# Eight matmuls on a tile of zeros ahead of all others on TensorE, in a transformer block on one core

## The chip, the cores and the metric

One Trainium2 chip, one of its cores. The metric is the device time of one execution in microseconds; before the change it is 1064.79 us (median of 3 runs). Of the core's engines the text uses TensorE (PE; its weight loads are PEld), VectorE (DVE), ScalarE (ACT), GpSimd (POOL) and SyncE (SP), which issues nearly all DMA transfers.

## The reference

One encoder block over 1024 tokens of width 1024, in float32. Two groups of eight heads share one input projection: group A is a sliding window with grouped keys, a distance penalty and a learned sink, group B attends to its own chunk of 64 tokens and eight chunks before it with a learned position bias. Cut to what is computed:

```python
n = rms_norm(h, norm1_g)
qa, ka, va, qb, kb, vb = split(n @ w_in)              # 512, 128, 128, 512, 512, 512 columns
ya = mixer_a(qa, ka, va, sinks)                       # window 128, 8 query heads on 2 key heads
yb = mixer_b(qb, kb, vb, rel_bias)                    # own chunk + 8 before
h = h + concat(rms_norm(ya, g_a), rms_norm(yb, g_b)) @ w_out
u = square(relu(rms_norm(h, norm2_g) @ w_ff1))        # 1024 -> 4096
h = h + u @ w_ff2
out = rms_norm(h, final_norm_g)
```

## The kernel before

Every float32 matrix is held as two tiles, a rounded high part and the low rest. A product is made of three matmuls in that form (`mm3`: high x high, high x low, low x high), each of 128x512 at most, summed in PSUM. All matmuls go through one helper, so they stand at line L146 of the profile (transposes at L149), and tiles tell them apart.

The order on TensorE is the order in which the code is written: while `pe_order["on"]` is set, the helper `pe` adds a dependency of each matmul on the one before. TensorE runs its instructions strictly in that order, so what the first waits for, all wait for. On the other engines a scheduler sets the order when the program is built; SP's loads keep the order of the code.

What the text needs is the beginning, the projections of group A, for tokens 0 to 511 (t = 0) and 512 to 1023 (t = 1):

- `load_xT` loads a slice of 128 channels of the transposed input (`xs`), ScalarE makes its high part and VectorE its low part (`nT`, L233 and L234), each times the gain `g1c`.
- `proj_weight` loads the weights of a head pair in four cuts (`st_kA`, `st_qA`), ScalarE makes the high part (L193), VectorE or GpSimd the low part (L152): `w_kA`, `w_qA`, `w_vA`.
- On TensorE `ip_kA` and `ip_qA` (keys and the first two query heads, t = 0) take turns, two channel slices or six matmuls at a time; then come `ip_vA` (24 matmuls), and the same three for t = 1.
- `token_scales` loads the tokens' rows (`xr`, a rotation of four buffers) and ScalarE squares and sums them; VectorE makes the scale `r` out of it (L162 to L169). `scales_along` spreads it along the free axis by four transposes on TensorE (tile `r`, a rotation of two PSUM banks), in the midst of `ip_kA` for t = 1, and ScalarE copies it to `R` (L251).
- `place` multiplies a projection by `R` into `ts_kA` or `ts_qA` on VectorE (L270, L272), has it split in high and low on ScalarE and another engine, and SP copies the parts by DMA to where the attention reads them (`KA`, `QA`; keys twice: eight copies).
- From 42 us on the attention of group A runs between more projections (`ip_qA` of the next head pairs). For one block of 128 queries: scores `S_A` on TensorE, bias and row maximum on VectorE (`P_A`, `nm_A`, L438), exponential on ScalarE (`P_A`, L439; sums with the sink: `es_A`), the division on GpSimd or VectorE (`P_A`, L545), transposes on TensorE (`pt_A`), their split on ScalarE and VectorE (`T_A`, L446 and L152), and the product with the values on TensorE (`av_A`).

The first matmuls are written so (accs are PSUM tiles, wts the weights):

```python
accs = [first_acc(n, 0) for n in range(3)]
for n, ks in [(n, (k, k + 1)) for k in range(0, NK, 2) for n in range(2)] + [(2, range(NK))]:
    project(accs[n], wts[n], 0, ks)
accs0, accs = accs, [first_acc(n, 1) for n in range(3)]
project(accs[0], wts[0], 1, (0, 1, 2))
scales_along(0)
turns = [first_place(n, 0, accs0[n]) for n in range(3)]
project(accs[0], wts[0], 1, range(3, NK))
project(accs[1], wts[1], 1)
```

After that come group B, the output projection, the two large products (`f` with w_ff1; `f_a`, `f_b`, `f_c` with w_ff2, each in a scheme of seven products of sums of quarters) and the final norm. The change does not touch them.

Of the kernel before, what the change touches and what calls it, by code (L numbers as in the profile page):

```python
# [8 lines left out]
F32 = mybir.dt.float32  # L9
F32R = mybir.dt.float32r  # L10
# [5 lines left out]
P = 128  # L16
# [4 lines left out]
HALF = 512  # L21
# [19 lines left out]
NEXT_AT = {(4, 2): (1, 2), (6, 4): (1, 1, 2, 2), (10, 4): (1, 3, 4, 7)}  # L41
POOL_NORM = ((1, 0), (1, 1))
PLAIN = (2, 3)


@with_exitstack
def kernel(
# [26 lines left out]
    nc = tc.nc  # L74
# [7 lines left out]
    def f(ap):  # L82
        return ap.bitcast(F32)

    def page(shape, name, dt=F32R):
        return main.tile(shape, dt, tag="pg", bufs=NPAGES, name=name)
# [32 lines left out]
    pe_order = {"on": False, "last": None}  # L119

    def pe(ins):

        if pe_order["on"]:
            if pe_order["last"] is not None:
                dep = mybir.DependencyInfo(mybir.DependencyClass.NoSync, mybir.DependencyReason.DATA)
                tc.add_manual_dep(ins.ins, pe_order["last"], dep, reason="program order")
            pe_order["last"] = ins.ins.name
# [17 lines left out]
    def matmul(*args, **kw):  # L145
        pe(nc.tensor.matmul(*args, **kw))  # L146
# [31 lines left out]
    def load_weight(src, shape, name, low_engine, cuts=1, pieces=1, gain=None):  # L178

        st = stage(shape, f"st_{name}")  # L180
        w = [page(shape, f"w{hl}_{name}") for hl in range(2)]

        def steps():
            n = shape[1] // cuts
            for i in range(0, shape[1], n):
                load(st[:, i : i + n], src[:, i : i + n])
                for j in range(i, i + n, n // pieces):
                    c = slice(j, j + n // pieces)
                    if gain is not None:
                        nc.scalar.activation(w[0][:, c], st[:, c], AF.Copy, scale=gain)  # L190
                        nc.vector.scalar_tensor_tensor(w[1][:, c], st[:, c], gain, f(w[0][:, c]), ALU.mult, ALU.subtract)
                        continue
                    nc.scalar.activation(w[0][:, c], st[:, c], AF.Copy)  # L193
                    width = shape[2] if len(shape) > 2 else 1
                    short = min(n // pieces, LOW_COLS // width) if low_engine is nc.gpsimd else n // pieces
                    for k in range(j, j + n // pieces, short):
                        c = slice(k, k + short)
                        split_l(low_engine, w[1][:, c], st[:, c], w[0][:, c])
                yield

        if cuts > 1:
            return w, steps()
        for _ in steps():
            pass
        return w
# [10 lines left out]
    sp_ = ExitStack()  # L216
    sp = sp_.enter_context(tc.tile_pool(name="sp", bufs=1))
    sps = sp_.enter_context(tc.tile_pool(name="sps", bufs=1, space=PSUM))
    r1 = cv.tile([P, TB], F32, name="r1")
    R1 = page([P, SEQ], "R1", F32)  # L220
    xT_src = xT.rearrange("(k p) s -> p k s", p=P)
# [71 lines left out]
    def proj_weight(c0, name, low_engine, *cuts):  # L293
        return load_weight(w_in[:, c0 : c0 + P].rearrange("(k p) c -> p k c", p=P), [P, NK, P], name, low_engine, *cuts)
# [44 lines left out]
            else:  # L339
                next(work)  # L340

    pe_order["on"] = True
    wk, k_steps = proj_weight(KA0, "kA", dve, 4)
    wq, q_steps = proj_weight(QA0, "qA0", dve, 4)
    load_steps([0, k_steps, 1, q_steps, 2, k_steps, 3, q_steps, 4, k_steps, 5, q_steps, 6, k_steps, 7, q_steps])
# [163 lines left out]
    class UnitA:  # L509
# [52 lines left out]
        def apply(self, u):  # L562
# [19 lines left out]
            for s in range(2):  # L582
                row = slice(s * HD, (s + 1) * HD)
                nc.scalar.activation(v(yc[row, c]), self.av[HD:, :, s, :], AF.Copy)
                if p.m in PLAIN:
                    nc.scalar.activation(v(ym[row, c]), self.av[:HD, :, s, :], AF.Copy)
                else:
                    nc.vector.tensor_tensor(v(ym[row, c]), self.av[:HD, :, s, :], v(yc[row, c]), ALU.add)
            if p.m in PLAIN:
                nc.gpsimd.tensor_tensor(ym[:, c], ym[:, c], yc[:, c], ALU.add)  # L590
# [82 lines left out]
    def split_y(y, src, m):  # L673

        if m not in PLAIN:
            gain = ogc[:, m : m + 1]
# [23 lines left out]
    def out_weight(m):  # L700

        return load_weight(w_out[m * P : (m + 1) * P, :], [P, D], f"o{m}", pool, 1, 2, ogc[:, m : m + 1] if m in PLAIN else None)

# [626 lines left out]
def build(arrays):  # L1330
    import concourse.bacc as _bacc

    nc = _bacc.Bacc("TRN2", target_bir_lowering=False, num_devices=1)
    args = [nc.dram_tensor(f"in_{n}_dram", arrays[n].shape, F32, kind="ExternalInput").ap() for n in _INS]
    args.append(nc.dram_tensor("out_0_dram", (SEQ, D), F32, kind="ExternalOutput").ap())
    with tile.TileContext(nc, schedule_with_timeline_sim=True) as tc:
        kernel(tc, *args)
    return nc
# [9 lines left out]
```

## Time and profile before

| | |
|---|---|
| median of 3 runs | 1064.79 us (1063.94 to 1064.91) |
| the profiled execution | 1064.61 us |
| its span, first to last instruction | 1062.5 us |
| TensorE busy | 1048.2 us, 99% of the span |
| first matmul starts | 5.04 us after the span's start |

A row of the profile has the line of the code, the engine and the operation, the tile written and the tiles read, the shape, and how many there are. A row in order of time starts with the start and the length in microseconds; in square brackets stands how long the engine had been idle before it, and what ended that. A row of waits has who waited for whom, the microseconds in total, how often, and the longest. A row of a stage has the busy time of PE, PEld, VectorE, ScalarE and GpSimd with the number of instructions started, the granted TensorE clock, the busy share of the DMA engines and GB/s. TensorE's matmuls overlap: the length of one row is longer than the step from one to the next.

### The profile page before, as it was taken

The numbers are of one execution on the slowest core, as the hardware profiler recorded it, in microseconds if no ns is written. First come the engines' busy times: TensorE is split into PE (matmuls) and PEld (weight loads), VectorE is DVE, ScalarE is ACT, GpSimd is POOL, SyncE is SP. The second block draws the span as 40 slices with busy tenths as digits, with TensorE's granted clock in tenths as the row PEclk, the third lists the DMA queues.
The fourth block names the chain that finished last, engine by engine and source line by source line (L and its number), as shares of the span: only waits on it lengthen the run. The fifth ranks groups of instructions, "written<-read, shape, count | busy, mean of one in ns | idle before, by whom it ended". The sixth has DMA issues, their size and how long they took to land.

```text
span 1062.5 us, 14416 instructions
## 1 busy us (share of the span) xinstructions
PE 1048.2 (99%) x5052; PEld 874.1 (82%) x5052; DVE 702.4 (66%) x1120; ACT 584.3 (55%) x1012; POOL 421.1 (40%) x326
## 2 busy tenths in 40 slices
PE   8999999999999999999999999999999999999997
PEld 6888888888888888888888888888888888888886
DVE  5577775767676765696534324436879877778667
ACT  7677786666574565675544554455533333333346
POOL 1476796334350243305564454345015024024026
PEclk9999999999999999999999999999999999999999
DMA  9954536253584442215544535416997535532004
GB/s 329 261 147 136 144 108 162 89 130 112 131 282 170 140 159 100 104 56 177 183 136 159 181 116 178 160 64 247 367 401 267 179 121 165 180 116 91 1 1 159
DMA packets 90440, 170.17 MB, mean 160 GB/s; under 512 B 7808, under 2 KB 43648, under 8 KB 90368
## 3 DMA queue, kind: packets, MB, share of 16 engines
q1 hardware_dynamic: 90080, 169.06, 48.1%
q8 instruction: 40, 0.66, 0.3%
q14 instruction: 32, 0.26, 0.1%
q10 hardware_dynamic: 288, 0.20, 0.1%
HBM read 105.26 MB, written 45.09 MB: 142 GB/s over the span
## 4 chain that ended last, share of the span: by engine, by line
PE 93%; DVE 3%; DMA 2%; ACT 1%; issue 1%; SPq 0%; DVEq 0%; ACTq 0%
PE f L146 27%; PE f_a L146 16%; PE f_c L146 8%; PE ip_qA L146 4%; PE op_B L146 4%; PE f_b L146 4%; PE ip_vB L146 4%; PE ip_qB L146 4%; PE op_A L146 4%; PE ip_kB L146 3%; PE av_B L146 3%; PE pt_B L149 2%; PE S_B L146 2%; PE S_A L146 1%; PE ip_kA L146 1%; PE av_A L146 1%
## 5 line engine op out<-in xcount | busy, mean ns | idle before, releaser
L146 PE MATMUL f<-X,W 128*128 128x512 f32 x1344 | 306.0, 389 | 0.1
L146 PEld LDWEIGHTS f<-X,W 128*128 128x128 f32 x1344 | 252.0, 188 | 52.9 <-DVE X L152 0.5
L146 PE MATMUL f_a<-V,U 128*128 128x512 f32 x756 | 173.6, 389 | 0.2 <-DVE bsf L137 0.2
L152 POOL TENSOR_TENSOR U<-u,U 128x1024 fp32r<-128x1024 f32 x32 | 80.4, 2512 | 226.9 <-PE f_c L146 134.9
L146 PEld LDWEIGHTS f_a<-V,U 128*128 128x128 f32 x756 | 141.9, 188 | 30.1 <-DVE bsf L137 0.6
L152 POOL TENSOR_TENSOR W<-T,W 128x1024 fp32r<-128x1024 f32 x29 | 75.6, 2609 | 141.6 <-ACT W L981 141.6
L146 PE MATMUL f_c<-V,U 128*128 128x512 f32 x384 | 88.4, 389 | 0.0
L146 PEld LDWEIGHTS f_c<-V,U 128*128 128x128 f32 x384 | 72.1, 188 | 15.0
L981 ACT ACTIVATE V<-Z 128x1024 fp32r<-128x1024 f32 x32 | 33.9, 1060 | 89.7 <-PE f_a L146 44.6
L1030 DVE TENSOR_TENSOR k<-f,k 128x1024 f32<-128x1024 f32 x24 | 29.3, 1221 | 60.7 <-PE f L146 60.7
L981 ACT ACTIVATE V<-w 128x1024 fp32r<-128x1024 f32 x24 | 25.4, 1060 | 78.9 <-issue 34.2
L152 POOL TENSOR_TENSOR W<-w,W 128x1024 fp32r<-128x1024 f32 x23 | 56.3, 2449 | 30.9 <-ACT W L981 30.8
L152 DVE TENSOR_TENSOR V<-w,V 128x1024 fp32r<-128x1024 f32 x24 | 47.6, 1985 | 27.1 <-ACT V L981 27.1
L981 ACT ACTIVATE U<-u 128x1024 fp32r<-128x1024 f32 x56 | 58.5, 1044 | 11.5 <-DMA ud<-k 7.1
L439 ACT ACTIVATE P_B<-P_B,nm_B 128x640 f32<-128x640 f32 (+2 forms) x64 | 44.3, 693 | 23.9 <-DVE nm_B L438 12.9
L1024 ACT ACTIVATE k<-f 128x1024 f32<-128x1024 f32 x24 | 24.6, 1026 | 59.1 <-PE f L146 59.1
L152 DVE TENSOR_TENSOR T_B<-pt_B,T_B 128x512 fp32r<-128x512 f32 (+2 forms) x72 | 39.7, 552 | 21.6 <-ACT T_B L446 21.3
L981 ACT ACTIVATE W<-T 128x1024 fp32r<-128x1024 f32 x32 | 33.9, 1058 | 35.5 <-PE f L146 21.1
L146 PE MATMUL ip_vB<-nT,w_vB 128*128 128x512 f32 x192 | 52.0, 399 | 0.9 <-DVE T_B L152 0.9
L146 PE MATMUL op_A<-w_o,y 128*128 128x512 f32 x192 | 52.2, 397 | 0.7 <-DVE h L773 0.4
L146 PE MATMUL ip_qB<-nT,w_qB 128*128 128x512 f32 x192 | 51.5, 396 | 0.0
L146 PE MATMUL ip_kB<-nT,w_kB 128*128 128x512 f32 x192 | 51.3, 396 | 0.0
(233 smaller groups left out, 2056.9 us busy)
## 6 DMA issues: line engine op xcount, KB each, us to landing
w<-in_w_ff_dram SPq DMA_DIRECT2D x64, 512.0 KB, 4.7
u<-ud SPq DMA_DIRECT2D x56, 512.0 KB, 4.7
ud<-k SPq DMA_DIRECT2D x48, 512.0 KB, 3.2
KkB<-ts_kB SPq DMA_DIRECT2D x64, 128.0 KB, 2.3
yd<-y SPq DMA_DIRECT2D x14, 512.0 KB, 2.8
y<-yd SPq DMA_DIRECT2D x14, 512.0 KB, 6.3
xs<-in_xT_dram SPq DMA_DIRECT2D x16, 256.0 KB, 5.3
xr<-in_x_dram SPq DMA_DIRECT2D x8, 512.0 KB, 7.0
```

Of the source, the lines that this page charges most:

```text
L146: pe(nc.tensor.matmul(*args, **kw))
L149: pe(nc.tensor.transpose(*args))
L152: engine.tensor_tensor(lo, full, f(hi), ALU.subtract)
L439: nc.scalar.activation(pr[:, :n], pr[:, :n], AF.Exp, bias=nm, scale=-1.0, accum_out=sm)
L981: nc.scalar.activation(w[0], full, AF.Copy)
L1024: nc.scalar.activation(kept[p], ps, AF.Copy)
L1030: dve.tensor_tensor(v, ps, v, ALU.add)
```

## The change

A tile `busy` of 128x512 zeros is made by a memset on VectorE. Eight matmuls multiply it by its own first 128 columns into a PSUM tile `idle_ps` that nothing reads. They are written ahead of all others, and the program order on TensorE is switched on ahead of them, not after them. `busy` takes a buffer of the rotation `xr`, `idle_ps` one of the rotation `r`. Later lines move down by 1 to 8 (in the order below L146 becomes L147, L234 becomes L242).

```diff
+EARLY = 8
...
     sps = sp_.enter_context(tc.tile_pool(name="sps", bufs=1, space=PSUM))
+    pe_order["on"] = True
+
+    busy = sp.tile([P, HALF], F32R, tag="xr", bufs=4, name="busy")
+    nc.vector.memset(f(busy), 0.0)
+    idle_ps = sps.tile([P, HALF], F32, tag="r", bufs=2, name="idle_ps")
+    for n in range(EARLY):
+        matmul(idle_ps, busy[:, :P], busy, start=n == 0, stop=n == EARLY - 1)
     r1 = cv.tile([P, TB], F32, name="r1")
...
-    pe_order["on"] = True
     wk, k_steps = proj_weight(KA0, "kA", dve, 4)
```

TensorE at the start of the program, before (each row is a matmul: line, tile written, tiles read, size of the result; the numbers are buffers):

```order
L146 MATMUL ip_kA_324<-nT_155,w_kA 128x512
L146 MATMUL ip_kA_324<-nT_159,w_kA 128x512
L146 MATMUL ip_kA_324<-nT_155,w_kA 128x512 x2
L146 MATMUL ip_kA_324<-nT_159,w_kA 128x512
L146 MATMUL ip_kA_324<-nT_155,w_kA 128x512
L146 MATMUL ip_qA_0_325<-nT_155,w_qA_183 128x512
```

and after:

```order
L147 MATMUL idle_ps<-busy 128x512 x8
L147 MATMUL ip_kA_335<-nT_166,w_kA 128x512
L147 MATMUL ip_kA_335<-nT_170,w_kA 128x512
L147 MATMUL ip_kA_335<-nT_166,w_kA 128x512 x2
L147 MATMUL ip_kA_335<-nT_170,w_kA 128x512
L147 MATMUL ip_kA_335<-nT_166,w_kA 128x512
L147 MATMUL ip_qA_0_336<-nT_166,w_qA_194 128x512
```

The eight stand ahead; the real matmuls keep their order, here and in the rest of the program. VectorE at the start, before:

```order
L94 MEMSET ones 128x1
L96 MEMSET eps_76 128x1
L234 SCALAR_TENSOR_TENSOR nT_159<-xs_185,g1c,nT_155 128x512
L152 TENSOR_TENSOR w_kA<-st_kA,w_kA 128x256
L234 SCALAR_TENSOR_TENSOR nT_159<-xs_185,g1c,nT_155 128x512
```

and after:

```order
L95 MEMSET ones 128x1
L97 MEMSET eps_76 128x1
L223 MEMSET busy 128x512
L242 SCALAR_TENSOR_TENSOR nT_170<-xs_196,g1c,nT_166 128x512
L153 TENSOR_TENSOR w_kA<-st_kA,w_kA 128x256
L242 SCALAR_TENSOR_TENSOR nT_170<-xs_196,g1c,nT_166 128x512
```

The memset comes third, ahead of the first low part; nothing else moves on VectorE, and nothing on ScalarE, GpSimd and SP but the numbers of buffers.

## What I predict

> **What bounds the kernel now.** I read the page first, for the engine that fills the span.
>
> ```profile
> span 1062.5 us, 14416 instructions
> PE 1048.2 (99%) x5052; PEld 874.1 (82%) x5052; DVE 702.4 (66%) x1120; ACT 584.3 (55%) x1012; POOL 421.1 (40%) x326
> PE 93%; DVE 3%; DMA 2%; ACT 1%; issue 1%; SPq 0%; DVEq 0%; ACTq 0%
> ```
>
> TensorE (PE) is busy for 99% of the span and makes up 93% of the chain that ended last. So the end can move only if TensorE's long row of matmuls moves as a whole. Next the list of what TensorE waited for, whole run:
>
> ```profile
> PE ip_kA L146 <- ACT w_kA L193: 5.0, 1, 5.0
> PE ip_vB L146 <- DVE T_B L152: 0.9, 1, 0.9
> ```
>
> The first row is the start: 5.0 us in which TensorE has nothing. That is the hole in which the change puts its matmuls. The second longest wait is 0.9 us. Third the chain of waits in order of time, for the first 60 us (start, length, what):
>
> ```profile
> 5.04 3.46 PE ip_kA L146 x6
> 8.51 2.56 PE ip_qA L146 x6
> 11.07 1.76 PE ip_kA L146 x6
> 12.83 1.37 PE ip_qA L146 x6
> 14.20 1.36 PE ip_kA L146 x6
> ...
> 19.64 5.44 PE ip_vA L146 x24
> ...
> 27.12 0.44 PE r L149 x4
> 27.56 3.43 PE ip_kA L146 x15
> ```
>
> All these matmuls but r have one shape, 128x512. Six of them take 2.56 us at 8.51 (427 ns each) and 1.36 us from 14.20 on (227 ns each), with no wait in either. The change of pace lies in the group of 1.76 us: 1.76 - 1.36 = 0.40 us is two slow steps (427 - 227 = 200 ns more each), so at about 11.8 us. The clock column of the stages does not show it:
>
> ```profile
> 8.00:9.00 1.00, 1.00 (x4) 0.81 (x3) 0.85 (x3) 0.87 (x2) 0.00 (x0) 1.00 0.98 336
> 17.00:18.00 1.00, 1.00 (x6) 0.84 (x5) 0.00 (x0) 0.86 (x3) 1.00 (x3) 1.00 1.02 410
> ```
>
> It gives 1.00 (the third figure from the end) for both stages, with x4 against x6 matmuls started; here the spacing is to be believed. TensorE thus begins at about half pace and gets its full pace some 6.7 us after its first matmul.
>
> **The change part by part.** It adds one memset on VectorE, eight matmuls 128x512 ahead of the first real one, and takes one of four xr buffers and one of two r banks for tiles that are used once; the orders of ScalarE, GpSimd and the DMA queue stay as they are. The operands of the start, each with its length:
>
> ```profile
> 0.84 0.06 DVE L96 MEMSET eps<- 128x1 f32 x1
> 4.59 0.40 ACT L193 ACTIVATE w_kA<-st_kA 128x256 fp32r<-128x256 f32 x1
> 4.72 0.75 DVE L234 SCALAR_TENSOR_TENSOR nT<-xs,g1c,nT 128x512 fp32r<-128x512 f32 x1 [3.83 <-ACT nT L233]
> 6.48 0.75 DVE L234 SCALAR_TENSOR_TENSOR nT<-xs,g1c,nT 128x512 fp32r<-128x512 f32 x1 [0.67 <-ACT nT L233]
> 8.31 2.76 PE L146 MATMUL ip_qA<-nT,w_qA 128*128 128x512 f32 x6
> 11.65 0.75 DVE L234 SCALAR_TENSOR_TENSOR nT<-xs,g1c,nT 128x512 fp32r<-128x512 f32 x1
> 14.62 0.42 DVE L152 TENSOR_TENSOR w_qA<-st_qA,w_qA 128x256 fp32r<-128x256 f32 x1
> 16.35 2.82 POOL L152 TENSOR_TENSOR w_vA<-st_vA,w_vA 128x256 fp32r<-128x256 f32 x4 [15.04 <-ACT w_vA L193]
> 25.09 0.17 DVE L169 RECIPROCAL r<-w_n 128x4 f32<-128x4 f32 x1
> 25.18 2.71 DVE L234 SCALAR_TENSOR_TENSOR nT<-xs,g1c,nT 128x512 fp32r<-128x512 f32 x4
> 26.96 0.60 PE L149 MATMUL r<-ident,r 128*128 128x128 f32 x4
> ```
>
> *The memset and the eight matmuls.* No row has a memset of 128x512 on VectorE. It costs more than the 128x1 one (0.06 us) and hardly more than an operation of that size that reads two tiles (0.75); I take 0.45, near the 0.42 of the pass over half the columns, because a memset reads nothing. VectorE is idle until 4.72 us (3.83 us of it shown in that row), so it hides. The memset runs from 0.90 to about 1.35; eight matmuls at the slow pace are 8 x 0.427 = 3.41 us, to about 4.8. The first real matmul waits for ScalarE until 4.59 + 0.40 = 4.99 anyway. At the upper bound of the memset the eight end at 5.1, 0.1 us too late. Cost taken: 0; ends kept: 0 to +0.1 us.
>
> *The buffers.* A used-once tile at the head of a rotation of four shifts every xr load by one buffer; each still follows the load four earlier, and the one that follows the zero tile comes long after 4.8 us. The same holds for the r banks. Nothing queues behind it: 0.
>
> *The faster start, at most.* If TensorE has its full pace from 5.04 on, 14 slow steps (6 + 6 + 2) could save 14 x 0.20 = 2.8 us. But the first six wait for operands: the fifth needs nT, ready at 6.48 + 0.75 = 7.23, so the six end at 7.23 + 0.05 + 2 x 0.227 = 7.73 where the next group begins at 8.31 now: 0.6 saved, not 1.2. The next eight save 1.6 us. Later operands (11.65 + 0.75 = 12.40, 14.62 + 0.42 = 15.04, the GpSimd pieces every 0.7 us from 16.35) come before they are needed even then. So ip_vA would start and end about 2.1 us earlier. Then the transposes r need the reciprocal of 25.09 + 0.17 = 25.26, which hangs on DMA and VectorE and not on TensorE: 26.96 - 25.3 = 1.6 us at most is carried past them.
>
> *What is late next.* I looked for every later operand in the first 60 us that does not itself come from TensorE. They lie here:
>
> ```profile
> 30.00:42.00 12.00, 12.00 (x59) 9.93 (x58) 4.73 (x12) 6.60 (x12) 5.22 (x9) 1.00 0.85 208
> 42.00:52.00 10.00, 10.00 (x55) 8.59 (x54) 6.59 (x22) 7.15 (x20) 6.18 (x8) 1.00 1.12 293
> 42.74 5.78 SPq L282 DMA_DIRECT2D KA<-ts_kA  x8
> SPq L282 <- DMA st_kB<-in_w_in_dram: 0.4, 1, 0.4
> 50.33 1.83 POOL L545 TENSOR_SCALAR P_A<-P_A,rc_A 128x256 f32<-128x256 f32 x2
> 53.23 0.38 PE L149 MATMUL pt_A<-ident,P_A 128*128 128x128 f32 x2
> 51.81 0.69 DVE L270 SCALAR_TENSOR_TENSOR ts_qA<-ip_qA,R 128x512 f32<-128x512 f32 x1 [0.67 <-DMA QA<-ts_qA]
> 52.82 0.48 DVE L438 CUSTOM_DVE_ANT_0 P_A<-S_A,b_A,nsink 128x256 f32<-128x256 f32 x1
> 53.61 0.49 ACT L439 ACTIVATE P_A<-P_A,nm_A 128x256 f32<-128x256 f32 x1
> 54.29 1.04 ACT L193 ACTIVATE w_qA<-st_qA 128x1024 fp32r<-128x1024 f32 x1
> 55.24 0.84 ACT L446 ACTIVATE T_A<-pt_A 128x256 fp32r<-128x256 f32 x2
> 55.63 0.42 DVE L152 TENSOR_TENSOR T_A<-pt_A,T_A 128x256 fp32r<-128x256 f32 x1
> 56.42 0.40 PE L146 MATMUL av_A<-T_A,VA 128*128 128x256 f32 x2
> ```
>
> The DMA engines are full from 42 to 52 us (share 1.12), with loads whose order and start do not depend on TensorE. The eight copies KA<-ts_kA stand in that queue and the last is issued at about 48, behind the load st_kB. VectorE stands still for 0.67 us until 51.81 because a ts buffer is still being read by those copies (the row names the DMA). Behind that ts_qA everything on VectorE and ScalarE stands in line, back to back: VectorE's P_A at 52.82, ScalarE's P_A at 53.61, w_qA at 54.29 to 55.33, T_A at 55.24, and VectorE's T_A from 55.63 to 56.05. The second av_A matmul (56.42 + 0.11 = 56.53) needs that T_A. So TensorE can be at most 56.53 - 56.05 = 0.48 us earlier there, less the lag from an operand's end to its matmul. That lag is 0.05 us at the start (4.99 to 5.04); I allow up to three times that here: 0.3 to 0.4. The pt_A transposes at 53.23 already cut the carry from 1.6 to about 1.1 (P_A is ready at 50.33 + 1.83 = 52.16).
>
> *Sum.* 2.1 gained at 20 us, 1.6 left at 27, 1.1 at 53, 0.3 to 0.4 at 56.5. I find no later place whose operand is not itself fed by TensorE, and carry 0.3 to the end; the bounds are 0 and 0.4 if the DMA row of the first 52 us stands as it is. The profiled execution took 1064.61 us (2.1 around its span); it becomes 1064.3. The median of the runs is 0.18 above that execution: 1064.79 - 0.3 = **1064.5**.
>
> [...]
>
> **The rivals.**
>
> *A, the whole start is carried.* If the copies KA<-ts_kA land earlier when ts_kA is ready earlier, the stop at 51.81 moves too. For it: share 0.85 between 30 and 42 us leaves some room. Against: the queue is full from 42, and the copies wait in it for the landing of loads ahead of them (st_kB). Then the carry past r stays: 1.4 to 1.6 us, time 1064.8 - 1.5 = 1063.3.
>
> *B, the change does nothing to the pace.* If eight matmuls on zeros do not bring the full pace before 11.8 us (the operands are zero, and the real ones behind them come with gaps until 8.3), TensorE is as slow as before: 1064.8, or 1064.9 with the 0.1 us of a late eighth matmul. If the pace changes at about 8.3, eight slow steps still save 1.6 us, more than the 0.4 that gets through, so the time is that of the forecast. [...]
>
> [...]
>
> **How the numbers follow.** Forecast (carry held to 0 to 0.4 us) 0.77; A 0.12; B 0.07; C 0.04. About 0.2%, or 2.1 us, is what a measurement can tell here from no change. Not even A reaches that by its middle, and the ceiling of 2.1 us only touches it; C stays below it too. With the scatter of the runs (1063.94 to 1064.91), I give faster 0.05, same 0.92, slower 0.03. The forecast's own range is 1064.4 to 1064.8, widened by the runs' scatter to 1063.8 - 1065.0. The range reaches to A below, 1063.3, and above over B with the scatter, to 1065.2; C and the ceiling are left out.
>
> **What would show it.** In the changed profile: eight idle_ps matmuls of 427 ns from about 1.4 to 4.8 us; ip_qA groups of six in 1.36 us from the first one (right) or 2.56 (B); ip_vA starting in the chain near 17.5 instead of 19.64; r near 25.4; then new rows in TensorE's waits, pt_A on GpSimd's P_A and av_A on VectorE's T_A, of some 0.5 us or more each; ts_qA on VectorE still at 51.8; the second av_A near 56.2. I am wrong if ts_qA moves with TensorE (A), or if a later wait of TensorE grows and gives back more than 0.3.

## The result, and the profile after

The changed kernel is slower by a little more than the runs can mistake for no change: 1066.86 us median of 9 runs (1065.23 to 1068.59) against 1064.27 of 9 runs of the kernel before beside them, ratio 1.0026 (95% interval 1.0017 to 1.0034; the ratios of this text are those on record, and not quite the quotients of the medians). The prediction was 1064.5 within 1063.3 to 1065.2. The profiled execution took 1066.43 us, 1.8 more than that of before.

First the page of the changed kernel, the span and the engines' busy time:

```profile
span 1064.4 us, 14424 instructions
PE 1050.6 (99%) x5060; PEld 874.8 (82%) x5060; DVE 699.9 (66%) x1121; ACT 584.9 (55%) x1012; POOL 422.7 (40%) x326
```

TensorE has 8 matmuls and 8 weight loads more, and 2.4 us more of busy time: less than the 3.8 us that the eight take, so the work behind them did get shorter. The start, in order of time (start, length):

```profile
0.97 0.48 DVE L223 MEMSET busy<- 128x512 f32 x1
1.51 3.78 PE L147 MATMUL idle_ps<-busy 128*128 128x512 f32 x8 [1.51 <-DVE busy L223]
5.09 2.25 PE L147 MATMUL ip_kA<-nT,w_kA 128*128 128x512 f32 x4
8.22 1.56 PE L147 MATMUL ip_qA<-nT,w_qA 128*128 128x512 f32 x6
9.62 1.53 PE L147 MATMUL ip_kA<-nT,w_kA 128*128 128x512 f32 x6
17.79 2.43 PE L147 MATMUL ip_vA<-nT,w_vA 128*128 128x512 f32 x10
```

The eight go ahead at the slow pace (3.78 us for all), the first real matmul starts at 5.09 (5.04 before), and groups of six are at full pace (1.5 us long by this view) from 8.22 on. In before the same view has the groups at 8.31 and 10.87 with 2.76 and 1.97. The trace's record of the granted clock puts the change at 6.88 us, against 11.74 before. So the front does what the change says: compared start by start, every matmul from 12 to 54 us comes about 1.7 us earlier than in before.

Then it is lost. Around 50 us:

```profile
25.27 0.60 PE L150 MATMUL r<-ident,r 128*128 128x128 f32 x4
51.54 0.38 PE L150 MATMUL pt_A<-ident,P_A 128*128 128x128 f32 x2
52.76 0.69 DVE L278 SCALAR_TENSOR_TENSOR ts_qA<-ip_qA,R 128x512 f32<-128x512 f32 x1 [2.28 <-DMA QA<-ts_qA]
54.57 0.71 PE L147 MATMUL S_A<-KA,QA 128*128 128x256 f32 x4 [1.52 <-DVE nm_A L445]
56.60 0.84 PE L147 MATMUL av_A<-T_A,VA 128*128 128x256 f32 x2
57.06 0.19 PEld L147 LDWEIGHTS av_A<-T_A,VA 128*128 128x128 f32 x1 [0.27 <-DVE T_A L153]
```

`pt_A` is still 1.7 us early. But VectorE's `ts_qA` starts at 52.76, not at 51.81 as before, after standing still for 2.28 us; TensorE waits 1.52 us for the work behind it, and the second `av_A` starts at 57.06 instead of 56.53: 0.53 us late. That 0.53 stays until 310 us. There it grows again, to 1.1 at 312, 1.35 at 313.4 and 2.38 at 316 (times of before), and 1.9 is left at the end. TensorE's list of waits, whole run:

```profile
PE S_A L147 <- DVE nm_A L445: 1.5, 1, 1.5
PE pt_B L150 <- DVE T_B L153: 1.3, 2, 1.2
PE ip_vB L147 <- DVE T_B L153: 0.9, 1, 0.9
```

The first two are new, one for each place; the third was there before. What stands behind each?

**Place 1: the last KA copy lands late.** `ts_qA` takes the buffer that the eight KA copies read. The last of the eight alone, in before and then in after (issue; then from issue to landing in us):

```profile
L282 SPq DMA_DIRECT2D KA<-ts_kA x1: 462/462/462, 48.1 to 48.1; - x1
DMA to landing us min/median/max: 3.5/3.5/3.5
```

```profile
L290 SPq DMA_DIRECT2D KA<-ts_kA x1: 462/462/462, 47.3 to 47.3; - x1
DMA to landing us min/median/max: 5.2/5.2/5.2
```

It is issued 0.75 us earlier and lands 0.95 later (52.54 against 51.59). The DMA traffic between 48 and 51.6 us has a queue in after that before does not have there:

```profile
q8 instruction: 1, 0.02, 2.2%
```

That queue carries 40 transfers of 16 KB over the run, one for about 250 of TensorE's 10,120 matmuls and weight loads on the mean (some 190 to 310 from one transfer to the next). By this count it is probably TensorE's own program being fetched; the page gives the queue's kind, `instruction`, and no engine. In before such a transfer comes at 55.0 us (51.5 when it was run again), when the copies have landed; with 16 instructions more, and TensorE 1.7 us early, it comes at 49.2, among them. TensorE's list has no wait for such a transfer, but at place 2a a copy lands 1.5 us later beside one (4.5 us in flight, not 3.0). That the transfer makes the last KA copy late is likely rather than shown: two of the kernels below have a transfer at 48.5 and 49.4 us, and their last copy takes 4.3 and 4.0 us, while sq4_before has none there and takes 4.2.

**Place 2a: the same at 299 us.** The transfer of `yd<-y`, in before and in after:

```profile
L505 SPq DMA_DIRECT2D yd<-y x1: 332/332/332, 297.3 to 297.3; - x1
DMA to landing us min/median/max: 3.0/3.0/3.0
```

```profile
L512 SPq DMA_DIRECT2D yd<-y x1: 332/332/332, 297.9 to 297.9; - x1
DMA to landing us min/median/max: 4.5/4.5/4.5
```

Its 128 packets of 4 KB start within 2.3 us of the issue in before; the instruction transfer begins at 2.3 us, just behind the last. In after it begins at 1.0 us and takes 1.45, and the last packets follow one another at 0.16 us, the length of one, until 3.8; that one of the 16 DMA engines served the transfer first is a guess (the trace does not name the engine of a packet). Behind `yd` in the queue stand `y<-yd` and the weights `st_o`, and ScalarE's `w_o` moves with them (before, then after):

```profile
307.02 1.34 ACT L190 ACTIVATE w_o<-st_o,ogc 128x512 fp32r<-128x512 f32 x2 [3.34 <-DMA st_o<-in_w_out_dram]
```

```profile
308.19 1.34 ACT L191 ACTIVATE w_o<-st_o,ogc 128x512 fp32r<-128x512 f32 x2 [3.92 <-DMA st_o<-in_w_out_dram]
```

The 1.17 us on ScalarE is 0.6 more than the 0.53 that was late already, and the `P_B` work behind it carries this to TensorE.

**Place 2b: VectorE stands behind GpSimd.** At 314 to 317 us, VectorE's `y` and GpSimd's `sqB`; before, then after:

```profile
314.30 0.75 DVE L678 SCALAR_TENSOR_TENSOR y<-Y,ogc,y 128x512 fp32r<-128x512 f32 x1
314.58 1.61 POOL L501 TENSOR_TENSOR sqB<-sqB,y 128x512 f32<-128x512 f32 x1
```

```profile
315.58 1.30 POOL L508 TENSOR_TENSOR sqB<-sqB,y 128x512 f32<-128x512 f32 x1
315.66 1.77 DVE L685 SCALAR_TENSOR_TENSOR y<-Y,ogc,y 128x512 fp32r<-128x512 f32 x1
```

The one that starts first, even by 0.08 us, has its normal length, and the other is longer: `y` by 1.02 us, or `sqB` by 0.31. In before VectorE is first, in after GpSimd is. `T_B` and TensorE's `pt_B` hang on `y`, so this microsecond is the second wait of the list. What the two share the traces do not say. Both orders come near to the second waiting for the first to end, by an estimate from these rows: a full wait would make `y` 1.30 - 0.08 + 0.75 = 1.97 us and `sqB` 0.75 - 0.28 + 1.30 = 1.77, and they take 1.77 and 1.61.

What sets the order lies four operations earlier on VectorE, at `ts_vB`; before, then after:

```profile
312.63 0.69 DVE L267 TENSOR_TENSOR ts_vB<-ip_vB,R 128x512 f32<-128x512 f32 x1
```

```profile
313.98 0.69 DVE L275 TENSOR_TENSOR ts_vB<-ip_vB,R 128x512 f32<-128x512 f32 x1 [0.34 <-DMA st_o<-in_w_out_dram]
```

VectorE stands still for 0.34 us that it does not lose in before, and `y` goes from 0.28 us ahead of `sqB` to 0.08 behind. In 12 of the 18 profiles of this text the stop is there, always 0.33 to 0.34 us (the view names now a DMA, now `S_B`), and `y` is behind; in the other six it is not, and `y` is ahead. Counting VectorE's instructions in the traces, its waits on semaphores included, the 12 have 704 or 705 of them ahead of `ts_vB` and the six 706 to 708. In the 12 the lost time lies behind the 703rd instruction, between two of those waits; in the six that place comes earlier, where VectorE waits for ScalarE's `padF` anyway. So the stop goes with a place in VectorE's instructions and not with the time. In after the count is 704 and in before 707: one memset more, and four waits on semaphores fewer. What VectorE does there the traces do not say; 11 of the 12 also take 0.42 to 0.48 us from a wait to the next instruction behind the 319th and the 1087th, 384 earlier and 384 later (3 in 100 such steps elsewhere are of that size).

### The profile page after: what moved, and what is told of

Read it like the earlier page. It is cut to its first block, busy times and chain, and to the rows that moved or that the text cites. A ratio compares the mean times of both kernels' runs of the same rounds, so it can differ in the third digit from the quotient of the medians.

```text
span 1064.4 us, 14424 instructions
## 1 busy us (share of the span) xinstructions
PE 1050.6 (99%) x5060; PEld 874.8 (82%) x5060; DVE 699.9 (66%) x1121; ACT 584.9 (55%) x1012; POOL 422.7 (40%) x326
## 4 chain that ended last, share of the span: by engine, by line
PE 86%; DMA 5%; DVE 4%; ACT 2%; POOL 1%; issue 1%; SPq 0%; DVEq 0%; ACTq 0%; POOLq 0%
PE f L147 27%; PE f_a L147 16%; PE f_c L147 8%; PE op_B L147 4%; PE f_b L147 4%; PE ip_qB L147 4%; PE op_A L147 4%; PE ip_kB L147 3%; PE ip_vB L147 3%; PE av_B L147 3%; PE pt_B L150 2%; PE S_B L147 2%; PE ip_qA L147 2%; DMA xs<-in_xT_dram 1%; PE av_A L147 1%; DMA b_A<-in_dist_dram 1%
## 5 line engine op out<-in xcount | busy, mean ns | idle before, releaser
L147 PE MATMUL f<-X,W 128*128 128x512 f32 x1344 | 305.9, 389 | 0.1
L147 PEld LDWEIGHTS f<-X,W 128*128 128x128 f32 x1344 | 251.9, 188 | 52.9 <-DVE X L153 0.5
L147 PE MATMUL f_a<-V,U 128*128 128x512 f32 x756 | 173.6, 389 | 0.2 <-DVE bsf L138 0.2
L147 PEld LDWEIGHTS f_a<-V,U 128*128 128x128 f32 x756 | 141.8, 188 | 30.1 <-DVE bsf L138 0.6
L147 PE MATMUL f_c<-V,U 128*128 128x512 f32 x384 | 88.4, 389 | 0.0
L147 PEld LDWEIGHTS f_c<-V,U 128*128 128x128 f32 x384 | 72.1, 188 | 15.0
L153 DVE TENSOR_TENSOR V<-w,V 128x1024 fp32r<-128x1024 f32 x24 | 50.5, 2104 | 29.9 <-ACT V L988 29.9
L988 ACT ACTIVATE V<-w 128x1024 fp32r<-128x1024 f32 x24 | 25.4, 1060 | 80.7 <-issue 34.3
L153 DVE TENSOR_TENSOR V<-Z,V 128x1024 fp32r<-128x1024 f32 x32 | 47.9, 1498 | 9.2 <-ACT V L988 5.9
L147 PE MATMUL ip_vB<-nT,w_vB 128*128 128x512 f32 x192 | 52.0, 399 | 0.9 <-DVE T_B L153 0.9
L147 PE MATMUL op_A<-w_o,y 128*128 128x512 f32 x192 | 52.1, 397 | 0.4 <-DVE h L780 0.4
L453 ACT ACTIVATE T_B<-pt_B 128x512 fp32r<-128x512 f32 (+2 forms) x72 | 34.9, 485 | 30.7 <-PE pt_B L150 30.5
```

The lines of the kernel that those rows point to most:

```text
L153: engine.tensor_tensor(lo, full, f(hi), ALU.subtract)
L453: nc.scalar.activation(T[:, 0, lo:hi], tp, AF.Copy)
L988: nc.scalar.activation(w[0], full, AF.Copy)
```

## The experiments

All have five rounds beside the kernel before on the same chip. Three theories were told apart: F, instruction transfers that fall on other DMA; E, the early clock alone; B, the buffers that the zero tiles take.

**The two kernels once more, and two ways to take E and B away.**

> The kernel before, for a second profile of it. All theories: 1064.3 us. Theory F: the instruction transfer of TensorE that lay at 55.0 us stays outside of 44 to 52 us, behind the copies, and ts_qA on VectorE starts near 51.8; if it falls on the copies in this execution, ts_qA comes late here too and this execution is about 1 us longer.

> The changed kernel once more, for a second profile. Theory F (instruction transfers): TensorE now starts early and is 16 instructions further on, so its 16 KB instruction transfer of about 49 us falls on the eight copies KA<-ts_kA, holds one of the 16 DMA engines for over 1 us, and the last copies land late. It expects about 1066.9 us, and in the profile either an instruction transfer between 46 and 52 us with VectorE's ts_qA after 52.3, or no such transfer and ts_qA near 51.0. Theory E (the early clock alone: TensorE ahead of its operands makes the later waits worse): about 1066.9 us, ts_qA late wherever that transfer lies. Theory B (the buffers: the zero tile and its bank shift two rotations): 1066.9, the same place lost every time.

```diff
-        matmul(idle_ps, busy[:, :P], busy, start=n == 0, stop=n == EARLY - 1)
+        matmul(idle_ps[:, :64], busy[:, :P], busy[:, :64], start=n == 0, stop=n == EARLY - 1)
```

> The eight added matmuls have 64 columns instead of 512: same instructions, same buffers, same memset, but TensorE is busy only a tenth as long before its first real matmul, so the clock should open as late as before (steps of 427 ns until 8.3 to 11.8 us). Theory E: no early clock, no loss: 1064.3 us, like the kernel before. Theory B: the loss stays: 1066.9. Theory F: the instruction transfers come 16 instructions (about 2 us) earlier than in the kernel before, the one at 55.0 at about 53, still behind the copies: 1064.3 to 1064.8, unless it falls on them.

The next puts the zeros into a page that a later `nT` tile fills, and the result into a bank that is free until then, so that no rotation shifts:

```diff
-    busy = sp.tile([P, HALF], F32R, tag="xr", bufs=4, name="busy")
+    busy = nT[1][1][3][:, 1]
-    idle_ps = sps.tile([P, HALF], F32, tag="r", bufs=2, name="idle_ps")
+    idle_ps = sps.tile([P, HALF], F32, tag="ip21", bufs=1, name="idle_ps")
```

> The eight matmuls of 128x512 stay, but the zeros lie in a page that is written only at 27 us (the last low part of the input, t = 1) and the result in the bank of ip_vA for t = 1; the rotations xr and r are as in the kernel before. Theory B: 1064.3 us or a little less, as the early clock then costs nothing. Theories E and F: as the changed kernel, about 1066.9 us.

Measured: before_again 1064.02 (ratio 0.9995, 0.9986 to 1.0005; one of its twelve executions, of 1800.68, is not in the ratio), after_again 1066.54 (1.0017, 1.0008 to 1.0027), tiny8 1066.96 (1.0022, 1.0012 to 1.0033), own_tiles 1065.75 (1.0013, 1.0003 to 1.0022). The loss is real and repeats. tiny8 has no early clock (full pace at 9.63 us; the kernel before, run again, had it at 9.45) and loses as much: E falls. Its transfer came at 50.1 us and not at about 53, so it does not tell F from B. own_tiles shifts no rotation and still loses, with the last KA copy 4.9 and `yd` 4.7 us in flight: B falls as the main cause. But `y` is first here, with 708 instructions of VectorE ahead of `ts_vB` and as many waits as in before, and the median is 0.8 us under that of after_again: for place 2b the buffers do count, by the waits that they bring.

**The wait of ts_qA taken away, and fewer or more instructions.** page_after gives `ts_kA` for t = 1 a buffer of its own, so that `ts_qA` need not wait; page_before does so in the kernel before.

```diff
-        elif name == "vA":
+        elif name == "vA" or (name == "kA" and t == 1):
             st = page([P, 2, HALF], f"ts_{name}_{t}")
```

> The changed kernel, with the ts tile of ip_kA for t = 1 in a page of its own, so that VectorE's next ts_qA need not wait for the eight copies KA<-ts_kA that read it. Theory F (the instruction transfer at 49 us holds those copies up, and through the buffer VectorE, ScalarE and the av_A matmuls): the loss at 56 us goes, ts_qA starts when its matmuls are done (about 49.5), TensorE keeps more of its 1.6 us until the scores S_A for the second half wait for the QA copies; 0.5 to 1.5 us less than the changed kernel's 1066.6, the loss near 310 us may stay: 1065.0 to 1066.0. Theory E (the early clock) and theory B (the buffers): no change from 1066.6.

> The same page in the kernel before. Theory F: a little faster than 1064.0, as the copies do not hold VectorE here either: 1063.3 to 1064.0. If 1066, the page does harm by itself and page_after tells nothing.

tiny4 is tiny8 with `EARLY = 4`, 8 extra instructions. less8_after is the changed kernel without eight of the matmuls of `ip_kB` for t = 0 (the product of the high weights with the low part of the tokens is left out, in all eight channel slices):

```diff
+            if short:
+                matmul(acc, w[0][:, k], n[0], start=k == 0, stop=False)
+                matmul(acc, w[1][:, k], n[0], start=False, stop=k == NK - 1)
+                continue
...
-                project(acc, w, t, (k,))
+                project(acc, w, t, (k,), name == "kB1" and t == 0)
```

> Four added matmuls of 64 columns: half the added instructions (8), no early clock. Theory F: TensorE's second instruction transfer comes near 50.5 to 51.5 us, at the end of the copies, and the one near 299 us still within the transfer yd<-y of 297 to 300 us: between the kernel before and the eight, 1064.5 to 1066.5, with executions of both kinds. Theory B: as with eight, 1066.9.

> The changed kernel with eight matmuls of ip_kB (second pair of group B, t = 0, about 150 us) left out: the products of the high weights with the low inputs. This takes 8 x 0.227 = 1.8 us of TensorE out and puts the count of TensorE's instructions behind that place back to that of the kernel before. Theory F: the transfer that lay at 298.9 us, 1 us after the start of yd<-y, comes about 1.6 us later against that copy, yd<-y lands after 3 us again instead of 4.5, and the 1.4 us lost near 310 us are not lost: 1066.6 - 1.8 - 1.4 = 1063.4. Without that cause (theory E or B): 1066.6 - 1.8 = 1064.8.

Measured: page_after 1066.13 (1.0021, 1.0012 to 1.003), page_before 1065.75 (1.0018, 1.0009 to 1.0027), tiny4 1065.34 (1.0017, 1.0008 to 1.0026), less8_after 1064.27 (1.0004, 0.9995 to 1.0013). The kernel before beside these four had 1063.60. In page_after `ts_qA` starts at 50.36 and no longer waits, but `S_A` still needs the last KA copy (5.5 us in flight) and comes at 54.65; the 0.5 to 1.5 us that were expected of it did not come. page_before loses its microsecond at 313 to 317 alone, where `y` came behind `sqB` (1.77 us) though nothing was added ahead of TensorE: so that pair of totals says nothing on the copies. less8_after removes as many instructions in the middle as the change adds at the start: place 1 loses as in after, a little less (last copy 5.1 us, `av_A` 0.2 us late), place 2 not at all (no instruction transfer near `yd`, 2.9 us in flight; `y` first, 0.75 us). Part of its time is the eight matmuls left out: 1.7 us by its trace at 152 us, of which 0.9 is given back by 159 us. Its total decides nothing: 1063.4 was expected if the transfers are the cause and 1064.8 if not, and 1064.27 lies between, 0.7 above the kernel before though it does less work.

**The same instructions, not at the start.** late8 is the kernel before with eight matmuls of 64 columns at 92 us, into a tile that the real ones then overwrite:

```diff
+            for n in range(8 if name == "kB0" and t == 0 else 0):
+                matmul(acc[:, :64], w[0][:, 0], nT[0][0][0][:, 0, :64], start=True, stop=True)
```

> The kernel before, with eight matmuls of 64 columns whose result is overwritten (operands of ip_kB itself, first column block) written at the head of ip_kB for t = 0, at about 92 us; nothing is added at the start, no zero tile. F (instruction transfers): the transfer at 55 us stays where it is in the kernel before (beyond 51 us), the last KA copy lands by 52.1 and S_A and av_A are within 0.1 us of the kernel before until 92 us; the eight cost 8 x 64 columns, about 0.2 to 0.5 us at 92; from there on the transfers stand as in the changed kernel (one at about 299 us, onto yd<-y, which then takes 4 to 5 us from issue to landing instead of 3.0), so with the flip of y and sqB the end is 1.0 to 2.3 us later, without the flip 0.5 to 1.2: 1064.5 to 1066.3. A theory in which the place at the head of the program matters, by the zero tile's buffers or by the start of the clock, says no loss beyond the 0.2 to 0.5 us of the eight themselves: 1064.1 to 1064.5, and yd<-y in 3.0 us.

Measured: 1066.35 (1.0021, 1.0012 to 1.0029), as slow as the changed kernel, with nothing at the start. Its last KA copy, its `yd<-y`, and its new wait of TensorE:

```profile
L282 SPq DMA_DIRECT2D KA<-ts_kA x1: 461/461/461, 47.6 to 47.6; - x1
DMA to landing us min/median/max: 4.1/4.1/4.1
```

```profile
L507 SPq DMA_DIRECT2D yd<-y x1: 332/332/332, 298.0 to 298.0; - x1
DMA to landing us min/median/max: 4.6/4.6/4.6
```

```profile
PE av_B L146 <- DVE padL L152: 1.0, 1, 1.0
```

At place 1 the transfer is at 54.6 us and `S_A` is not late (53.87 us against 54.50 in before: 0.6 us early, with nothing added ahead of it); at place 2 a transfer comes 0.9 us after the issue of `yd`, and TensorE waits. `y` came first here (0.75 us), so 2a alone brings TensorE from 0.5 us late after the eight to 2.0 late at the end of this profile. Two misses: the eight took 0.8 us at 92, not 0.2 to 0.5, and with `y` first 0.5 to 1.2 us were expected in all where the medians differ by 2.4. A few rows on VectorE and in SP's queue also change order in this kernel. The theory that the place at the head of the program matters falls. Over all profiles the last KA copy is 3.5 to 4.2 us in flight in the five kernels without instructions added at the start, and 4.5 to 5.5 in eleven of the thirteen with them (4.0 and 4.3 in the other two).

**GpSimd's sqB cut in four.** So that VectorE need wait for a quarter only. The first try cut the tile of m = 7 (at 373 us), not the one at 315:

```diff
-                nc.gpsimd.tensor_tensor(acc, acc, y2, ALU.add)
+                w = HALF // 4 if self.m == 7 else HALF
+                for i in range(0, HALF, w):
+                    nc.gpsimd.tensor_tensor(acc[:, i : i + w], acc[:, i : i + w], y2[:, i : i + w], ALU.add)
```

> The changed kernel, with the one GpSimd operation acc += y2 of the last group-B tile (sqB<-sqB,y, 128x512, 1.3 to 1.6 us) cut into four of 128 columns; the results are the same and the orders of all other engines too. If VectorE's y<-Y,ogc,y (0.75 or 1.77 us) is long because it has to wait for the GpSimd operation that began 0.08 us ahead of it, it need wait for a quarter only: y takes 0.75 to 1.2 us, pt_B's wait for T_B shrinks by 0.5 to 1.0 and the time is 0.5 to 1.0 us below the changed kernel's, 1065.5 to 1066.3. If y's length has another cause (its own operands, yd's landing), it stays near 1.77 and the time at 1066.5 to 1066.9. The losses at 50 us (+0.5 at av_A) and at yd<-y stay in both cases.

> The same cut of sqB<-sqB,y in the kernel before, as the control. There VectorE's y starts ahead of sqB in the one profile and behind it in another; where it is ahead, nothing is to be gained: 1063.7 to 1064.3, within 0.1% of the kernel before. If the cut costs GpSimd time that TensorE sees, it is slower by 0.3 us or more.

> The changed kernel with both mends: ts_kA for t = 1 in a page of its own, so that ts_qA on VectorE does not wait for the KA copies, and sqB<-sqB,y cut in four. If both sites are as the traces read: ts_qA does not wait for the copies any more, av_A at +0.1 to +0.3 against the kernel before (S_A still needs the last KA), yd<-y still late (0.7 us), y's 1.0 us mostly gone: 1064.6 to 1065.6. If the sites are only symptoms of something else that makes the changed kernel slower, it stays at 1066.1 to 1066.9.

Measured: 1067.28 (1.0033, 1.0021 to 1.0046; six runs), 1064.0 (1.0, 0.9991 to 1.0008), 1065.86 (1.0015, 1.0006 to 1.0024). The row at 315 us is uncut in all three, and `y` takes 1.77, 0.75 and 1.76 us; they serve as repeats of after, before and page_after. With `m == 6 and t == 0` in the condition the cut is at the right tile:

> The changed kernel, with the GpSimd operation sqB<-sqB,y of the third tile of group B for t = 0 (at 315.6 us, 128x512, 1.3 us) cut into four of 128 columns (each about 0.46 us by such pieces elsewhere); the orders on the other engines are unchanged. If VectorE's y<-Y,ogc,y is long because a GpSimd operation that began just ahead holds it up, it takes 0.75 to 1.3 us instead of 1.77, and TensorE's pt_B gets T_B 0.5 to 1.0 us earlier: 1065.5 to 1066.3. If y's length has another cause: y near 1.77, time 1066.5 to 1067.3.

> The same cut, and ts_kA for t = 1 in a page of its own, so that VectorE's ts_qA does not wait for the KA copies. The late last KA copy and the late yd<-y stay, as far as the instruction transfers fall on them. If the cut works: 1064.8 to 1065.8, below page_after's 1066.13 by 0.4 to 1.0. If not: 1065.8 to 1066.6.

Measured: cut_after 1065.69 (1.0017, 1.0008 to 1.0025), cut_page_after 1065.15 (1.0011, 1.0002 to 1.002). VectorE and GpSimd in cut_after:

```profile
315.66 1.74 POOL L510 TENSOR_TENSOR sqB<-sqB,y 128x128 f32<-128x128 f32 x3
315.74 0.93 DVE L687 SCALAR_TENSOR_TENSOR y<-Y,ogc,y 128x512 fp32r<-128x512 f32 x1
```

GpSimd is again first by 0.08 us, and `y` now takes 0.93 us: the length of `y` is a wait for the GpSimd operation in front. cut_after is 1.9 us above the kernel before beside it, the changed kernel 2.6. What is left is `yd<-y`, 4.5 and 4.6 us in flight in the two kernels.

**The busy stretch with half the instructions.** Two matmuls on the zeros as plain float32 stand as four in the trace and take as long (3.78 us in fp2_cut_page, 3.69 in fp2_after):

```diff
-EARLY = 8
+EARLY = 2
-        matmul(idle_ps, busy[:, :P], busy, start=n == 0, stop=n == EARLY - 1)
+        matmul(idle_ps, f(busy[:, :P]), f(busy), start=n == 0, stop=n == EARLY - 1)
```

> The changed kernel with two matmuls on the zero tile instead of eight, read as plain float32 and not as fp32r; the order on every engine is otherwise the same, and TensorE runs 4 (or, if a float32 matmul is several instructions in the trace, up to 16) extra instructions instead of 16. F (instruction transfers): with 4, the transfer at 49 to 50 us moves to 52 us or later, the last KA copy lands by 52.1 instead of 52.5 and S_A and av_A come 0.2 to 0.6 us earlier than in the kernel before; if the transfer at 299 us misses yd too the end is 1063.2 to 1064.2, with y behind sqB up to 1065.2. With 16 instructions all is as after. A theory in which the zero tile, its buffers or the early clock makes the loss says 1066 to 1067 here too.

> All mends together: two float32 matmuls on zeros, ts_kA for t = 1 in its own page, sqB<-sqB,y cut in four. If the losses are the three that the traces show, this one keeps the gain at the front as far as S_A and av_A let it through: 1062.8 to 1064.0. If it is 1065 or more, a loss is left that is not understood.

Measured: fp2_after 1065.91 (1.0019, 1.001 to 1.0028), fp2_cut_page 1064.31 (1.0002, 0.9993 to 1.001). fp2_after keeps its gain through both transfers: its last KA copy takes 4.0 us, `yd` 2.9, and TensorE is 0.4 to 1.1 us early from 54 to 313 us. Then `y` comes behind `sqB`, and a microsecond goes. Its profiled execution, 1064.72, is at the low end of its runs, whose median is above what was expected, so the runs hold something that this one profile does not show. One expectation failed: a transfer still came at 49.4 us and did not make the last copy late. With all three mends the time is that of the kernel before, above the 1062.8 to 1064.0 that were expected: the gain at the front is not kept. Its last KA copy is still late, with 5.3 us in flight; `ts_qA` does not wait for it. `yd` and `y` there:

```profile
L514 SPq DMA_DIRECT2D yd<-y x1: 333/333/333, 296.9 to 296.9; - x1
DMA to landing us min/median/max: 2.8/2.8/2.8
```

```profile
314.27 0.93 DVE L687 SCALAR_TENSOR_TENSOR y<-Y,ogc,y 128x512 fp32r<-128x512 f32 x1
```

No version beat the kernel before.

**All kernels at place 2.** The columns are the median, us in flight of `yd<-y`, and the length of `y`, the last two from the one profile of each; the kernel before beside them was at 1063.6 to 1064.3:

| kernel | median us | yd | y |
|---|---|---|---|
| before (beside after) | 1064.27 | 3.0 | 0.75 |
| before_again | 1064.02 | 2.9 | 0.75 |
| sq4_before | 1064.00 | 2.8 | 0.75 |
| less8_after | 1064.27 | 2.9 | 0.75 |
| fp2_cut_page | 1064.31 | 2.8 | 0.93 |
| page_before | 1065.75 | 2.8 | 1.77 |
| tiny4 | 1065.34 | 3.0 | 1.76 |
| fp2_after | 1065.91 | 2.9 | 1.77 |
| own_tiles | 1065.75 | 4.7 | 0.75 |
| late8 | 1066.35 | 4.6 | 0.75 |
| cut_after | 1065.69 | 4.5 | 0.93 |
| cut_page_after | 1065.15 | 4.6 | 0.94 |
| after | 1066.86 | 4.5 | 1.77 |
| after_again | 1066.54 | 5.1 | 1.76 |
| tiny8 | 1066.96 | 4.5 | 1.76 |
| page_after | 1066.13 | 4.4 | 1.77 |
| sq4_after | 1067.28 | 4.8 | 1.77 |
| sq4_page_after | 1065.86 | 4.5 | 1.76 |

Neither late (`y` counts as late from 1.7 us): 1064.0 to 1064.3. One of the two late: 1065.2 to 1066.4. Both: 1065.9 to 1067.3. The last two overlap, and less8_after owes part of its place to the matmuls that it leaves out. This orders the times; that each is a cause rests on cut_after and on page_before (`y`), and on late8 and the packets of `yd`. What each is worth is less sure: in the one profile of late8 a late `yd` alone brings 1.3 us, and in after it brings 0.6.

## Why the prediction was wrong

- **The memset and the eight matmuls at no cost: right.** 0.48 us for the memset (0.45 forecast), the first real matmul 0.05 us late (0 to 0.1).
- **The pace: right in kind, smaller in size.** Full pace from 6.9 us, not from 5.04, which the forecast had assumed; 1.7 us were gained at 20, not 2.1. And 2.3 of the 4.9 us by which the full pace comes earlier need not come from the change: the kernel before has it at 11.74 us in one profile and at 9.45 in the other, and tiny8 at 9.63. What sets this time within an execution was not shown.
- **r: right; pt_A: no bound.** `r` at 25.27 (25.4 forecast). `pt_A` was 1.7 us early, where 1.1 was forecast: GpSimd's `P_A`, put at an end of 52.16, ended at 51.50.
- **"with loads whose order and start do not depend on TensorE": the step that failed.** The order is as before, but one traffic does depend on TensorE: by its count the fetch of its own instructions (at 49.2 us here, at 55.0 in before), the likely cause here. `ts_qA` was put at 51.81 as a fixed point; it was at 52.76, and 0.3 to 0.4 us of gain at `av_A` became 0.53 of loss. The forecast kept that row fixed and looked only for what could be saved against it.
- **"I find no later place whose operand is not itself fed by TensorE": failed too.** Such a search finds data, not an instruction transfer beside a copy (`yd` 4.5 us in flight, not 3.0), nor `y` behind GpSimd's `sqB` (1.77 us, not 0.75). In this profile TensorE loses 0.6 us by `yd` (0.53 late to 1.11), 0.2 by the stop at `ts_vB` (to 1.35) and 1.0 by `y` behind `sqB` (to 2.38).
- **"Nothing queues behind it: 0", for the buffers: failed as well.** No load came later by them, but with the two rotations VectorE has four waits fewer ahead of `ts_vB`, and that moved its stop of 0.34 us to where it puts `y` behind `sqB`. own_tiles, without the shift, has as many waits as before, and `y` first.
- **The rivals.** C came near the measured time by a fall back to the slow pace, which was an estimate and did not happen: in after the record of the granted clock has full speed from 6.88 to 1061.6 us, and the groups of six take 1.5 us each from 8.22 us on. A fell with `ts_qA`; B fell with the row of 8.22.

The chances were worked out from cases that could end outside the runs' scatter only by the pace of TensorE; a case in which a shift of a microsecond costs more than it gains, by work that does not hang on its data, was not among them.

**What stays open.** What VectorE does in its stop of 0.34 us. What the runs of fp2_after hold beside their profile. Where the line lies for `yd`: a transfer 0.9 to 1.1 us after its issue always made it late; at 2.2 to 2.7 us it did in six kernels (three or fewer of the packets, or the landing itself, came behind it) and in six it did not. And how much of the end belongs to place 1: cut_page_after is 0.5 us under cut_after, but their intervals overlap.

## What to carry to other kernels

On a kernel whose bound engine is full to 99%, a gain at the front is worth only what the next fixed operand lets through; and that operand's time must be asked for again once the shift moves other traffic, instruction transfers included (at 49.2 us here, not at 55.0). Before believing a change of 0.2%, look for operations of VectorE and GpSimd that start within a few tenths of each other on the critical chain, since one instruction or wait more or fewer on VectorE can swap them for a microsecond, as from 705 to 706 here; cutting the GpSimd one into pieces bounds the loss (`y` 0.93 us, not 1.77). Few and long filler instructions on the fullest engine did better here: fp2_cut_page, with four of them in the trace for eight, is 0.8 us under cut_page_after.

## What the runs showed of the hardware

The 16 KB transfers, by their count probably TensorE's program, take 0.9 to 1.9 us each in before and after, and a 512 KB copy (`yd`) whose last packets come behind one lands 1.4 to 2.1 us late. VectorE's 128x512 operation with two tiles to read takes 0.75 us alone and 1.77 behind a GpSimd operation of that size that began 0.08 us ahead; behind one of 128 columns it takes 0.93. From VectorE's 703rd to its 704th instruction it takes 0.42 to 0.45 us in all 12 profiles in which two waits stand there, and an operation behind them comes 0.33 to 0.34 us later for it.
